# Latent attention: one two-bank score tile, one maximum and one exponential a token tile, and the gates multiplied straight from PSUM

## The chip, the cores and the metric

The kernel runs on one core of a Trainium2 chip. The metric is the device time of one execution in microseconds (us), and lower is better. Three runs of the kernel before gave 3876.71, 3877.76 and 3880.07 us; their median is 3877.76 us.

## The reference, cut to what matters

The whole program is two blocks of two layers each. The first block has a long convolution layer and a grouped attention layer, each followed by an expert layer. The second block has a layer that joins a recurrent unit with a latent attention, and then a state-space layer. The change concerns the latent attention of the second block alone:

```
def _mla_attention(q_nope, q_rope, k_nope, k_rope, v):
    for blk in range(seqlen // Q_BLOCK):              # 8 blocks of 128 tokens
        q0, kend = blk * Q_BLOCK, blk * Q_BLOCK + Q_BLOCK
        s = (einsum('bqhd,bkhd->bhqk', q_nope[:, q0:kend], k_nope[:, :kend])
             + einsum('bqhr,bkr->bhqk', q_rope[:, q0:kend], k_rope[:, :kend])) * scale
        s = where(causal mask, s, -inf)
        p = softmax(s, axis=-1)
        outs.append(einsum('bhqk,bkhd->bqhd', p, v[:, :kend]))
    ...
    y = concatenate([y_rnn, y_mla], axis=-1) * silu(gate)
```

There are 1024 tokens, 8 heads, 64 + 32 columns of query and key a head, and 64 of value. The attention is causal: the tokens of tile t, 128 of them, see (t + 1) x 128 keys.

## The kernel before, in words

Matrices are kept in fp32 and multiplied in three passes: each operand is split into a high part (rounded) and a low part (what is left), and high x high, high x low and low x high are summed. K.split (lines 127 to 134) writes the high part on ScalarE and the low part on VectorE, or on GpSimd where that is asked for.

`mla_attend` (line 1709) runs over 8 heads. For each head it splits the 96-row query and key (line 1722; GpSimd makes the low parts for every head but the first), and then goes over the token tiles in the order 4, 5, 6, 7, 0, 1, 2, 3. Tiles 4 to 7 are the second group of 512 tokens, tiles 0 to 3 the first.

For one tile, `mla_tile` (line 1737) works in parts of 512 keys: one part for tiles 0 to 3, two for tiles 4 to 7. Each part has a PSUM tile of one bank (512 fp32 a partition), from a pool of four (`s=(1, 4)`, line 2260). Three matmuls a part give the scores, and one more with a bf16 mask adds the causal mask on the diagonal block (line 1750). VectorE takes the maximum of each part (line 1755) and, for two parts, the maximum of the two columns, negated (line 1758). ScalarE takes the exponential of each part with that maximum as bias, and writes the part's sum to a column of `sm` (line 1761). `sm` has two rows a tile, one for each part; the second row of tiles 0 to 3 is set to zero (line 1727).

`mla_pT` (line 1764) transposes the tile's probabilities on TensorE, four blocks to a PSUM bank of the pool `tp` (three banks), and splits them into a high part (ScalarE) and a low part (VectorE).

After the last tile of a group, `mla_out` (line 1776) loads the gates of this head and group into the one buffer `ag` (line 1781, on the queue of SP, where the load has to wait until the buffer's last reader is done). It adds the two rows of sums (line 1783), takes reciprocals (line 1784), and turns these columns into rows by four transposes into a `tp` bank (line 1786). ScalarE copies them out of PSUM (line 1788) and GpSimd multiplies them with the gates (line 1789). TensorE multiplies probabilities and values into the one bank of `ov`, ScalarE copies the upper half out (line 1797), VectorE adds the lower (line 1798), GpSimd multiplies with the gated reciprocals (line 1799), and the result is stored over the gates in DRAM (line 1800).

Each engine runs its instructions in one fixed order. The order is not the program's: a planner simulates the engines when the program is built (line 2346, `schedule_with_timeline_sim=True`) and puts each engine's instructions into the order in which they become ready there, earlier program lines first; `K.first(20)` (line 1757) moves an instruction ahead. A buffer taken again waits for all users of the tile that held it (`reuse_waits="tile"`). Heads therefore overlap, and the loads and splits of the next stage's weights (`ProjNorm.weights`, line 1822, tiles `raw`, `pwh`, `pwl`) are placed among the last heads.

Of the kernel before, what the change touches and what calls it, by code (L numbers as in the profile page):

```python
# [10 lines left out]
F32 = mybir.dt.float32  # L11
# [4 lines left out]
OP = mybir.AluOpType  # L16
# [1497 lines left out]
class Ab:  # L1514
# [194 lines left out]
    def mla_attend(self, cp, wk, yT):  # L1709
        K, nc = self.K, self.K.nc  # L1710
        V, G = nc.vector, nc.gpsimd
        idb = cp.tile([P, P], BF16, name="idb")
        V.tensor_copy(out=idb, in_=K.ident)
        z = cp.tile([P, P], BF16, name="zb")
        G.memset(z, 0.0)
        msk = cp.tile([P, P], BF16, name="mskb")
        G.affine_select(out=msk, in_=z, pattern=[[-1, P]], compare_op=OP.is_ge, fill=-1e30, base=0, channel_multiplier=1)
        for h in range(8):
            qk = [wk.tile([96, T], F32R, name=n, tag=n) for n in ("aqh", "aql", "akh", "akl")]
            for s in (slice(0, T),) if h else (slice(0, 512), slice(512, T)):  # L1720
                for i, x in ((2, self.kT), (0, self.qT)):
                    K.split(qk[i][:, s], qk[i + 1][:, s], x[h // 4][0:96, h % 4, s], lo_eng="pool" if h else "dve")
            pp = []
            for tg in range(2):
                pp.append([cp.tile([P, 4 + 4 * tg, 512], F32R, name=f"ap{x}{tg}") for x in "hl"])
            sm = K.small.tile([P, 2, NT], F32, name="asm", tag="asm", bufs=2)
            G.memset(sm[:, 1, 0:4], 0.0)
            todo = [4, 4]
            for t in (4, 5, 6, 7, 0, 1, 2, 3):
                p = self.mla_tile(wk, qk, t, idb, msk, sm)  # L1730
                q = t // 4
                self.mla_pT(p, pp[q], t)
                todo[q] -= 1
                if not todo[q]:
                    self.mla_out(wk, yT, h, q, *pp[q], sm[:, :, 4 * q:4 * q + 4])

    def mla_tile(self, wk, qk, t, idb, msk, sm):

        K, nc = self.K, self.K.nc
        qh, ql, kh, kl = qk  # L1740
        n = (t + 1) * P
        ts = slice(t * P, n)
        parts = []
        for o in range(0, n, 512):
            e = max(o + 256, min(n, o + 512))
            ps = K.psum("as", "s")
            for q, (x, y) in enumerate(((qh, kh), (qh, kl), (ql, kh))):
                K.mm(ps[:, 0:e - o], x[:, ts], y[:, o:e], q == 0, q == 2 and e < n)
            if n <= o + 512:
                K.mm(ps[:, t * P - o:n - o], idb, msk, False, True)  # L1750
            parts.append((o, min(512, n - o), ps))
        m = len(parts)
        mx = K.small.tile([P, 3], F32, name="amx", tag="amx")
        for j, (o, w, ps) in enumerate(parts):
            nc.vector.tensor_reduce(out=mx[:, j:j + 1], in_=ps[:, 0:w], axis=AX.X, op=OP.max, negate=m == 1)
        if m == 2:
            with K.first(20):
                nc.vector.tensor_reduce(out=mx[:, 2:3], in_=mx[:, 0:2], axis=AX.X, op=OP.max, negate=True)
        p = wk.tile([P, 512 * m], F32, name="aprob", tag=f"aprob{m}", bufs=2)
        for j, (o, w, ps) in enumerate(parts):  # L1760
            nc.scalar.activation(out=p[:, o:o + w], in_=ps[:, 0:w], func=AF.Exp, bias=mx[:, 2 * m - 2:2 * m - 1], accum_out=sm[:, j, t:t + 1])
        return p

    def mla_pT(self, p, pp, t):
# [11 lines left out]
    def mla_out(self, wk, yT, h, tg, ph, pl, sm):  # L1776

        K, nc = self.K, self.K.nc
        gt = wk.tile([64, 512], F32, name="ag", tag="ag", bufs=1)
        dst = yT.piece(512 + h * 64, 512 + h * 64 + 64, tg * 512, (tg + 1) * 512)  # L1780
        nc.sync.dma_start(out=gt, in_=dst)
        rs = K.small.tile([P, 4], F32, name="ars", tag="ars", bufs=2)
        nc.vector.tensor_tensor(out=rs, in0=sm[:, 0], in1=sm[:, 1], op=OP.add)
        nc.vector.reciprocal(out=rs, in_=rs)
        rp = K.psum("rT", "tp")
        columns_to_rows(K, rp, rs)
        r = wk.tile([64, 512], F32, name="arb", tag="arb", bufs=1)
        nc.scalar.activation(out=r, in_=rp[0:64, 0:512], func=AF.Copy)
        nc.gpsimd.tensor_tensor(out=gt, in0=r, in1=gt, op=OP.mult)
        po = K.psum("ao", "ov")  # L1790
        nk = tg * 4 + 4
        for k in range(nk):
            c0 = max(0, k - tg * 4) * P
            K.mm(po[:, c0:512], self.v[:, k, h], ph[:, k, c0:512], k == 0, False)
            K.mm(po[:, c0:512], self.v[:, k, h], pl[:, k, c0:512], False, k == nk - 1)
        o = wk.tile([64, 512], F32, name="aoh", tag="aoh", bufs=1)
        nc.scalar.activation(out=o, in_=po[64:128, 0:512], func=AF.Copy)
        nc.vector.tensor_tensor(out=o, in0=po[0:64, 0:512], in1=o, op=OP.add)
        nc.gpsimd.tensor_tensor(out=o, in0=o, in1=gt, op=OP.mult)
        nc.sync.dma_start(out=dst, in_=o)  # L1800
# [439 lines left out]
def recurrent_mla(K, hD, x2D, yT, x0):  # L2240
    ab = Ab(K)
    a = K.a
    with ExitStack() as st:
        with K.staged("right", n=1024, bufs=3), K.pool("mlc", 1, side="right") as lp:
            with K.banks(mm=(2, 2), rg=(2, 1), tp=(1, 2)):
                with K.pool("rnw", 1) as wp, K.pool("u2", 1) as up, K.pool("abv", 1) as vp:
                    uh = up.tile([P, KT, T], F32R, name="uh")
                    ul = up.tile([P, KT, T], F32R, name="ul")
                    with K.pool("mlw", 1, side="right") as lw, K.pool("mp1", 1, side="right") as rp, K.pool("mp2", 2) as wk, K.pool("fn", 1) as fn:
                        w = load_w(K, lw, a["ab_w_in_2"][0], 1536, 416, KT, "m")  # L2250
                        ab.mla_tables(lp, rp)
                        first_norm(K, fn, hD, a["final_norm_g"], uh, ul, x2D, lambda t: t % 2 and ab.mla_latent(w, wk, uh, ul, t - 1), bufs=3, gp=lw, x0=x0)
                    ab.vectors(vp)
                    ab.gate_weights(vp)
                    with K.pool("rnk", 2) as wk:
                        ab.rnn(wk, wp, yT, uh, ul)
            ap = [st.enter_context(K.pool(f"mla{i}", 1)) for i in range(3)]
            with K.banks(mm=(2, 2), tp=(1, 4)), K.pool("mp3", 1) as rp, K.pool("mp4", 2) as wk:
                ab.mla_heads(ap, rp, wk)
        with K.banks(s=(1, 4), tp=(1, 3), ov=(1, 1)), K.pool("mac", 1, side="right") as cp, K.pool("mat", 2, side="right") as wk:  # L2260
            ab.mla_attend(cp, wk, yT)


# [86 lines left out]
```

## Time and profile before

| what | value |
|---|---|
| median of three runs | 3877.76 us |
| the profiled execution | 3875.91 us, span 3874.2 us |
| TensorE busy | 3539.8 us (91%) |
| VectorE busy | 2812.6 us (73%) |
| ScalarE busy | 2082.9 us (54%) |
| GpSimd busy | 1057.2 us (27%) |
| mean granted TensorE clock | 0.959 of full speed |

The profile is one execution, taken by the hardware profiler. Times in it are counted from the first instruction. PE is TensorE's matmuls, PEld its weight loads, DVE is VectorE, ACT is ScalarE, POOL is GpSimd, and SP is the engine whose queue issues the loads and stores. An instruction is named by its line, its operation and "out<-in" with the program's tile names: `as` are scores, `amx` maxima, `aprob` exponentials, `apT`, `aph` and `apl` the transposed probabilities and their parts, `asm` and `ars` the sums and their reciprocals, `rT` and `arb` the reciprocals as rows, `ag` the gates, `ao` and `aoh` the output. In brackets stands how long the engine was idle before an instruction, and what ended it; of several waits the profile names the one that it takes for the last.

### The profile page before, as it was taken

To read this page: it belongs to the slowest core of one execution; us is meant where nothing else is said; L and a number is where in the kernel's file an instruction comes from. 1 tells how busy PE (TensorE), PEld (TensorE's weight loads), DVE (VectorE), ACT (ScalarE), POOL (GpSimd) and SP (SyncE) were. 2 spreads that over 40 slices of the span, in tenths; PEclk is the share of its full clock that TensorE was granted. 3 is DMA by queue.
4 is the path that set the end of the run, shared out by engine and by line. 5 is a ranking of instruction groups with operands and counts; after the bars stand their busy time and mean duration, and the time that the engine had idled before them with its cause. 6 is when DMAs were issued, how large, how long until landed. Compare 5 with 4: busy or idle time off the path is not lost.

```text
span 3874.2 us, 52781 instructions
## 1 busy us (share of the span) xinstructions
PE 3539.8 (91%) x19679; PEld 3004.9 (78%) x19679; DVE 2812.6 (73%) x4848; ACT 2082.9 (54%) x3228; POOL 1057.2 (27%) x939
## 2 busy tenths in 40 slices
PE   7997999985999989899895999979998999999998
PEld 6885878764988979777785988878876877778777
DVE  6547878857988779777777988866476856665565
ACT  4334532222776763689824776754486138665520
POOL 2004755400353321244401453322353000000010
PEclk9998999987999999999997999989999999999999
DMA  4223233454999961000265999951113313232431
GB/s 155 95 83 109 112 132 121 132 200 166 356 361 353 357 221 41 16 12 12 65 225 211 371 354 356 361 177 44 48 34 102 118 41 97 85 95 66 146 139 63
DMA packets 221321, 603.64 MB, mean 156 GB/s; under 512 B 23350, under 2 KB 129704, under 8 KB 195465
## 3 DMA queue, kind: packets, MB, share of 16 engines
q1 hardware_dynamic: 209369, 558.59, 40.0%
q0 software_dynamic: 11696, 41.69, 4.1%
q8 instruction: 155, 2.54, 0.3%
q14 instruction: 101, 0.83, 0.1%
HBM read 503.60 MB, written 96.60 MB: 155 GB/s over the span
## 4 chain that ended last, share of the span: by engine, by line
PE 59%; DVE 11%; ACT 5%; DMA 4%; issue 3%; POOL 1%; SPq 0%; ACTq 0%; DVEq 0%; POOLq 0%
PE out L176 12%; PE gate L176 8%; PE xbc L176 7%; PE up L176 5%; DVE mwl L134 4%; PE down L176 4%; PE z L176 3%; PE ov L176 2%; PE pT L125 2%; PE gs L176 2%; PE as L176 1%; PE yd L176 1%; PE qk L176 1%; PE xr L176 1%; POOL mwl L134 1%
## 5 line engine op out<-in xcount | busy, mean ns | idle before, releaser
L134 DVE TENSOR_TENSOR mwl<-mwr,mwh 128x1024 fp32r<-128x1024 f32 x486 | 644.4, 1377 | 54.5 <-ACT mwh L130 53.6
L130 ACT ACTIVATE mwh<-mwr 128x1024 fp32r<-128x1024 f32 x576 | 562.9, 1050 | 52.6 <-PE up L176 28.8
L134 POOL TENSOR_TENSOR mwl<-mwr,mwh 128x1024 fp32r<-128x1024 f32 x90 | 257.5, 2887 | 271.1 <-ACT mwh L130 252.7
L1857 POOL DMA_DIRECT2D pyr<-y3T_d x31 | 23.5, 758 | 725.2 <-PE z L176 592.2
L1226 POOL DMA_INDIRECT xg<-xn_d,idx x32 | 58.9, 1839 | 466.9 <-DVE gsc L1224 466.3
L915 POOL TENSOR_TENSOR oh<-oh,oh 64x256 f32<-64x256 f32 (+1 forms) x56 | 55.0, 983 | 396.8 <-ACT oh L914 382.4
L134 DVE TENSOR_TENSOR gpl<-pT,gph 128x512 fp32r<-128x512 f32 x168 | 110.7, 685 | 40.6 <-ACT gph L130 26.7
L125 PE MATMUL pT<-ident,prob 128*128 128x128 f32 x896 | 126.7, 276 | 13.9 <-DVE gpl L134 8.6
L873 DVE TENSOR_REDUCE mx<-gs 128x1 f32<-128x1024 f32 x96 | 117.0, 1218 | 30.4 <-PE gs L176 30.0
L176 PE MATMUL gate<-mwh,xgl 128*128 128x384 f32 x512 | 137.2, 349 | 0.6 <-DVE xgl L134 0.4
L125 PEld LDWEIGHTS pT<-ident,prob 128*128 128x128 f32 x896 | 105.2, 141 | 39.9 <-ACT prob L875 6.6
L176 PE MATMUL gate<-mwl,xgh 128*128 128x384 f32 x512 | 134.7, 343 | 0.9 <-DVE mwl L134 0.8
L176 PE MATMUL out<-pwh,pyl 128*128 128x512 f32 x384 | 121.8, 398 | 13.6 <-DVE pyl L134 13.6
L176 PE MATMUL gate<-mwh,xgh 128*128 128x384 f32 x512 | 134.0, 341 | 0.0
L176 PE MATMUL up<-mwl,xgh 128*128 128x384 f32 x512 | 132.0, 337 | 1.9 <-DVE mwl L134 1.9
L176 PE MATMUL up<-mwh,xgh 128*128 128x384 f32 x512 | 132.2, 338 | 0.0
L176 PE MATMUL up<-mwh,xgl 128*128 128x384 f32 x512 | 131.6, 337 | 0.0
L130 ACT ACTIVATE xgh<-xgT 128x512 fp32r<-128x512 f32 (+1 forms) x68 | 38.1, 566 | 173.5 <-PE xgT L125 172.9
L176 PE MATMUL down<-mwl,hh 128*128 128x512 f32 x384 | 122.6, 401 | 6.1 <-POOL mwl L134 6.0
L176 PE MATMUL down<-mwh,hl 128*128 128x512 f32 x384 | 122.9, 400 | 0.0
L176 PE MATMUL out<-pwh,pyh 128*128 128x512 f32 x384 | 121.8, 398 | 0.0
L176 PE MATMUL out<-pwl,pyh 128*128 128x512 f32 x384 | 121.6, 398 | 0.0
(743 smaller groups left out, 11366.0 us busy)
## 6 DMA issues: line engine op xcount, KB each, us to landing
mwr<-in_exp_w_gate_dram SPq DMA_DIRECT2D x64, 1536.0 KB
mwr<-in_exp_w_up_dram SPq DMA_DIRECT2D x64, 1536.0 KB
mwr<-in_exp_w_down_dram SPq DMA_DIRECT2D x64, 1536.0 KB
raw<-in_ssd_w_in_dram SPq DMA_DIRECT2D x40, 512.0 KB
csr<-cs_d SPq DMA_DIRECT2D x32, 512.0 KB
k_d<-kev SPq DMA_DIRECT2D x54, 256.0 KB
kt<-k_d SPq DMA_DIRECT2D x54, 256.0 KB
raw<-in_hy_w_in_dram SPq DMA_DIRECT2D x10, 1024.0 KB
```

What stands on the lines that cost most here:

```text
L125: self.nc.tensor.transpose(out, in_, self.ident[:n, :n])
L130: nc.scalar.activation(out=hi, in_=src, func=AF.Copy)
L134: e.tensor_tensor(out=lo, in0=src, in1=hi.bitcast(F32), op=OP.subtract)
L176: self.nc.tensor.matmul(out=out, lhsT=lhsT, rhs=rhs, start=start, stop=stop)
L873: nc.vector.tensor_reduce(out=mx, in_=ps, axis=AX.X, op=OP.max, negate=True)
L915: nc.gpsimd.tensor_tensor(out=o2, in0=o2, in1=o, op=OP.add)
L1226: nc.gpsimd.indirect_dma_start(out=xg, out_offset=None, in_=self.xnD, in_offset=bass.IndirectOffsetOnAxis(ap=idx[:, 0:1], axis=0))
L1857: K.nc.gpsimd.dma_start(out=raw, in_=yT[q].rearrange("(p k) t -> p k t", k=self.kt)[:, :, t * P:(t + 1) * P])
```

## The change

Tiles 4 to 7 get one PSUM tile of two banks each, from a pool of two (`s=(2, 2)`); tiles 0 and 1 share one such tile, a bank each, and so do tiles 2 and 3. The matmuls are the same and write the same number of columns. One maximum and one exponential then go over the whole width of a tile, up to 1024 columns in two banks. The sums need one row, so the memset and the addition go. VectorE multiplies the transposed reciprocals with the gates straight out of PSUM, in place of ScalarE's copy and GpSimd's multiply.

```diff
-            sm = K.small.tile([P, 2, NT], F32, name="asm", tag="asm", bufs=2)
-            G.memset(sm[:, 1, 0:4], 0.0)
-            todo = [4, 4]
+            sm = K.small.tile([P, NT], F32, name="asm", tag="asm", bufs=2)
             for t in (4, 5, 6, 7, 0, 1, 2, 3):
-                p = self.mla_tile(wk, qk, t, idb, msk, sm)
+                if t > 3 or t % 2 == 0:
+                    ps = K.psum("as", "s")
+                p = self.mla_tile(wk, qk, t, idb, msk, sm, ps if t > 3 else ps[:, t % 2 * 512:t % 2 * 512 + 512])
                 q = t // 4
                 self.mla_pT(p, pp[q], t)
-                todo[q] -= 1
-                if not todo[q]:
-                    self.mla_out(wk, yT, h, q, *pp[q], sm[:, :, 4 * q:4 * q + 4])
+                if t % 4 == 3:
+                    self.mla_out(wk, yT, h, q, *pp[q], sm[:, 4 * q:4 * q + 4])
...
         for o in range(0, n, 512):
             e = max(o + 256, min(n, o + 512))
-            ps = K.psum("as", "s")
             for q, (x, y) in enumerate(((qh, kh), (qh, kl), (ql, kh))):
-                K.mm(ps[:, 0:e - o], x[:, ts], y[:, o:e], q == 0, q == 2 and e < n)
+                K.mm(ps[:, o:e], x[:, ts], y[:, o:e], q == 0, q == 2 and e < n)
             if n <= o + 512:
-                K.mm(ps[:, t * P - o:n - o], idb, msk, False, True)
-            parts.append((o, min(512, n - o), ps))
...
-        for j, (o, w, ps) in enumerate(parts):
-            nc.vector.tensor_reduce(out=mx[:, j:j + 1], in_=ps[:, 0:w], axis=AX.X, op=OP.max, negate=m == 1)
-        if m == 2:
-            with K.first(20):
-                nc.vector.tensor_reduce(out=mx[:, 2:3], in_=mx[:, 0:2], axis=AX.X, op=OP.max, negate=True)
-        p = wk.tile([P, 512 * m], F32, name="aprob", tag=f"aprob{m}", bufs=2)
-        for j, (o, w, ps) in enumerate(parts):
-            nc.scalar.activation(out=p[:, o:o + w], in_=ps[:, 0:w], func=AF.Exp, bias=mx[:, 2 * m - 2:2 * m - 1], accum_out=sm[:, j, t:t + 1])
+                K.mm(ps[:, t * P:n], idb, msk, False, True)
+        mx = K.small.tile([P, 1], F32, name="amx", tag="amx")
+        nc.vector.tensor_reduce(out=mx, in_=ps[:, 0:n], axis=AX.X, op=OP.max, negate=True)
+        p = wk.tile([P, 1024 if t > 3 else 512], F32, name="aprob", tag=f"aprob{t // 4}", bufs=2)
+        nc.scalar.activation(out=p[:, 0:n], in_=ps[:, 0:n], func=AF.Exp, bias=mx, accum_out=sm[:, t:t + 1])
...
-        nc.vector.tensor_tensor(out=rs, in0=sm[:, 0], in1=sm[:, 1], op=OP.add)
-        nc.vector.reciprocal(out=rs, in_=rs)
+        nc.vector.reciprocal(out=rs, in_=sm)
         rp = K.psum("rT", "tp")
         columns_to_rows(K, rp, rs)
-        r = wk.tile([64, 512], F32, name="arb", tag="arb", bufs=1)
-        nc.scalar.activation(out=r, in_=rp[0:64, 0:512], func=AF.Copy)
-        nc.gpsimd.tensor_tensor(out=gt, in0=r, in1=gt, op=OP.mult)
+        nc.vector.tensor_tensor(out=gt, in0=rp[0:64, 0:512], in1=gt, op=OP.mult)
...
-        with K.banks(s=(1, 4), tp=(1, 3), ov=(1, 1)), K.pool("mac", 1, side="right") as cp, K.pool("mat", 2, side="right") as wk:
+        with K.banks(s=(2, 2), tp=(1, 3), ov=(1, 1)), K.pool("mac", 1, side="right") as cp, K.pool("mat", 2, side="right") as wk:
```

## Rows read from the trace of the kernel before

**Rows 1.** The page: its first line.

```profile
span 3874.2 us, 52781 instructions
```

**Rows 2.** Busy time by head period: stretch, us, then PE, PEld, DVE, ACT, POOL; clock; DMA.

```profile
2833.28:2851.98 18.70, 18.36 (x119) 14.96 (x117) 14.39 (x36) 16.37 (x43) 10.11 (x8) 1.00 0.20 57
...
2869.71:2887.34 17.63, 16.85 (x114) 14.22 (x113) 14.16 (x35) 15.69 (x43) 9.94 (x8) 1.00 0.13 32
...
2922.60:2949.72 27.12, 20.21 (x112) 15.98 (x111) 19.49 (x40) 19.30 (x46) 15.15 (x8) 0.87 0.32 98
```

**Rows 3.** Waits of TensorE in the stage: us in total, times, longest.

```profile
PE as L176 <- ACT aprob L1761: 10.5, 7, 6.2
```

**Rows 4.** TensorE in time, steady head: start, us, instruction [idle before].

```profile
2879.14 0.23 PE L176 MATMUL as<-mskb,idb 128*128 128x128 bf16 x1
...
2883.26 0.44 PE L176 MATMUL as<-akh,aqh 96*128 96x384 f32 x1 [0.78 <-ACT aprob L1761]
```

**Rows 5.** ScalarE in time, steady head.

```profile
2877.81 0.59 ACT L1788 ACTIVATE arb<-rT 64x512 f32<-64x512 f32 x1
...
2878.28 0.59 ACT L130 ACTIVATE aph<-apT 128x512 fp32r<-128x512 f32 x1
...
2882.43 0.69 ACT L1761 ACTIVATE aprob<-as,amx 128x512 f32<-128x512 f32 x1
...
2883.09 0.70 ACT L1761 ACTIVATE aprob<-as,amx 128x512 f32<-128x512 f32 x1
...
2883.75 0.38 ACT L1761 ACTIVATE aprob<-as,amx 128x128 f32<-128x128 f32 x1
```

**Rows 6.** VectorE in time, steady head.

```profile
2879.86 0.68 DVE L1755 TENSOR_REDUCE amx<-as 128x1 f32<-128x512 f32 x1
...
2880.66 0.14 DVE L1758 TENSOR_REDUCE amx<-amx 128x1 f32<-128x2 f32 x1
```

**Rows 7.** ScalarE, TensorE and GpSimd in time, the period from 2922.60.

```profile
2939.66 1.06 ACT L130 ACTIVATE pwh<-raw 128x1024 fp32r<-128x1024 f32 x1 [4.37 <-DMA raw<-in_ab_w_out_dram]
...
2943.30 0.69 PE L176 MATMUL as<-akh,aqh 96*128 96x384 f32 x1 [6.18 <-ACT aprob L1761]
...
2929.41 4.46 POOL L1799 TENSOR_TENSOR aoh<-aoh,ag 64x512 f32<-64x512 f32 x1 [0.90 <-POOL asm L1727]
```

**Rows 8.** ScalarE in time, the other attention of the kernel.

```profile
1703.74 1.10 ACT L875 ACTIVATE prob<-gs,mx 128x1024 f32<-128x1024 f32 x1
...
1704.83 0.58 ACT L130 ACTIVATE gph<-pT 128x512 fp32r<-128x512 f32 x1
```

**Rows 9.** Groups by form, 2815 to 2978: busy us, mean ns; idle before.

```profile
L1755 DVE TENSOR_REDUCE amx<-as 128x1 f32<-128x512 f32 x48 | 32.5, 681 | 6.7 <-PE as L176 6.7
...
L1798 DVE TENSOR_TENSOR aoh<-ao,aoh 64x512 f32<-64x512 f32 x15 | 10.1, 675 | 2.5 <-ACT aoh L1797 2.4
...
L1783 DVE TENSOR_TENSOR ars<-asm 128x4 f32<-128x4 f32 x16 | 5.7, 359 | 1.6 <-ACT aprob L1761 1.1
...
L1758 DVE TENSOR_REDUCE amx<-amx 128x1 f32<-128x2 f32 x32 | 4.5, 140 | 0.3
```

**Rows 10.** The page's group of 1024-wide maxima, the other attention.

```profile
L873 DVE TENSOR_REDUCE mx<-gs 128x1 f32<-128x1024 f32 x96 | 117.0, 1218 | 30.4 <-PE gs L176 30.0
```

**Rows 11.** GpSimd, then the DMA queue, in time, steady head.

```profile
2876.51 1.26 POOL L1799 TENSOR_TENSOR aoh<-aoh,ag 64x512 f32<-64x512 f32 x1 [0.90 <-POOL asm L1727]
...
2881.15 1.28 POOL L1789 TENSOR_TENSOR ag<-arb,ag 64x512 f32<-64x512 f32 x1 [3.37 <-ACT aprob L1761]
...
2878.30 0.60 SPq L1781 DMA_DIRECT2D ag<-yT  x1
...
2884.47 0.60 SPq L1781 DMA_DIRECT2D ag<-yT  x1
```

**Rows 12.** VectorE in time, the stage's tail.

```profile
2973.54 1.02 DVE L1783 TENSOR_TENSOR ars<-asm 128x4 f32<-128x4 f32 x1
...
2978.55 0.68 DVE L1798 TENSOR_TENSOR aoh<-ao,aoh 64x512 f32<-64x512 f32 x1 [2.74 <-ACT aoh L1797]
```

More of the change, by code (lines that the diff above doesn't have):

```diff
@@ L1725, in mla_attend, with mla_tile @@
                 pp.append([cp.tile([P, 4 + 4 * tg, 512], F32R, name=f"ap{x}{tg}") for x in "hl"])
-            sm = K.small.tile([P, 2, NT], F32, name="asm", tag="asm", bufs=2)
-            G.memset(sm[:, 1, 0:4], 0.0)
-            todo = [4, 4]
+            sm = K.small.tile([P, NT], F32, name="asm", tag="asm", bufs=2)
             for t in (4, 5, 6, 7, 0, 1, 2, 3):
-                p = self.mla_tile(wk, qk, t, idb, msk, sm)
+                if t > 3 or t % 2 == 0:
+                    ps = K.psum("as", "s")
+                p = self.mla_tile(wk, qk, t, idb, msk, sm, ps if t > 3 else ps[:, t % 2 * 512:t % 2 * 512 + 512])
                 q = t // 4
                 self.mla_pT(p, pp[q], t)
-                todo[q] -= 1
-                if not todo[q]:
-                    self.mla_out(wk, yT, h, q, *pp[q], sm[:, :, 4 * q:4 * q + 4])
-    def mla_tile(self, wk, qk, t, idb, msk, sm):
+                if t % 4 == 3:
+                    self.mla_out(wk, yT, h, q, *pp[q], sm[:, 4 * q:4 * q + 4])
+    def mla_tile(self, wk, qk, t, idb, msk, sm, ps):
         K, nc = self.K, self.K.nc
@@ L1742, in mla_tile @@
         ts = slice(t * P, n)
-        parts = []
         for o in range(0, n, 512):
             e = max(o + 256, min(n, o + 512))
-            ps = K.psum("as", "s")
             for q, (x, y) in enumerate(((qh, kh), (qh, kl), (ql, kh))):
-                K.mm(ps[:, 0:e - o], x[:, ts], y[:, o:e], q == 0, q == 2 and e < n)
+                K.mm(ps[:, o:e], x[:, ts], y[:, o:e], q == 0, q == 2 and e < n)
             if n <= o + 512:
-                K.mm(ps[:, t * P - o:n - o], idb, msk, False, True)
-            parts.append((o, min(512, n - o), ps))
-        m = len(parts)
-        mx = K.small.tile([P, 3], F32, name="amx", tag="amx")
-        for j, (o, w, ps) in enumerate(parts):
-            nc.vector.tensor_reduce(out=mx[:, j:j + 1], in_=ps[:, 0:w], axis=AX.X, op=OP.max, negate=m == 1)
-        if m == 2:
-            with K.first(20):
-                nc.vector.tensor_reduce(out=mx[:, 2:3], in_=mx[:, 0:2], axis=AX.X, op=OP.max, negate=True)
-        p = wk.tile([P, 512 * m], F32, name="aprob", tag=f"aprob{m}", bufs=2)
-        for j, (o, w, ps) in enumerate(parts):
-            nc.scalar.activation(out=p[:, o:o + w], in_=ps[:, 0:w], func=AF.Exp, bias=mx[:, 2 * m - 2:2 * m - 1], accum_out=sm[:, j, t:t + 1])
+                K.mm(ps[:, t * P:n], idb, msk, False, True)
[3 more added lines that the diff above has]
+        nc.scalar.activation(out=p[:, 0:n], in_=ps[:, 0:n], func=AF.Exp, bias=mx, accum_out=sm[:, t:t + 1])
         return p
```

## The prediction, made before the result was known

> **What bounds the kernel now.** I read the head of the page first, then the attention stage by head, then the waits of TensorE there, then each engine's instructions in order of time through one steady head. The span is 3874.2 us [rows 1]; the profiled execution took 3875.91 us, so 1.71 us lie around the span, and it stands 1.85 us under the median of the runs shown (3877.76). The change touches one stage, the latent attention, from 2815 to 2978 us, some 160 us or 4% of the span. Whatever the change does, it can only give back what TensorE loses there.
>
> Cut at the four transposes of each head's first reciprocals, the stage falls into head periods [rows 2]. Three periods in a row are 17.63 us (one of them is shown) with TensorE busy 16.85, ScalarE 15.69, VectorE 14.16, GpSimd 9.94. TensorE is the pace, idle 0.78 us a head, and ScalarE is close behind. Two periods are odd: the first takes 18.70, and the one from 2922.60 takes 27.12, 9.49 over a steady one. Over the stage TensorE waits 10.5 us for an exponential before a score matmul, 7 times [rows 3], its longest wait by far.
>
> In a steady head that wait has one place [rows 4]: the scores of tile 2 (96x384) stand 0.78 us for a bank that tile 7 still holds. The bank comes free with the exponential of tile 7's first half, started 2882.43, its second half at 2883.09 [rows 5]. That exponential was not waiting for its maximum, ready at 2880.80 [rows 6]; ScalarE did a copy of an output half and two splits of transposes first.
>
> The 27.12 us period has another cause: ScalarE stands 4.37 us for the next stage's raw weights, with exponentials queued behind it, and TensorE stands 6.18 us for one of these [rows 7]. The weights' DMA was late because the output multiply on GpSimd took 4.46 us there [rows 7] instead of 1.26 [rows 11].
>
> **The change, part by part.** TensorE keeps every matmul and transpose, so its 16.85 us a head are untouched.
>
> *ScalarE.* Four tiles a head (4 to 7) lose one of two exponentials, one accumulator read with it. For tile 7 the two halves take 2 x 0.66 = 1.32 us from start to start [rows 5]; one 1024-wide exponential with its read takes 1.09 in the other attention of this kernel (1703.74 to 1704.83) [rows 8]. That saves 0.23; the same fixed part goes from tiles 4 to 6, so 4 x 0.23 = 0.92 a head. The two copies of the reciprocals out of PSUM go: 0.47 from start to start [rows 5], so 0.94. Together 1.86 us of ScalarE's 15.69 a head.
>
> *VectorE.* A 512-wide maximum costs 681 ns, the two-column one 140 [rows 9], a 1024-wide one 1218 [rows 10]. Tile 7: 681 + 681 + 140 - 1218 = 284 saved; what goes in tiles 4 to 6 is the same, one instruction's fixed part and the two-column one. Four tiles: 1.14 us. The two additions of partial sums go, 2 x 0.359 = 0.72. The gate multiply comes, twice; its nearest row is the 64x512 addition of the output halves, which also has one operand in PSUM, 675 ns [rows 9], so 1.35. Net 0.5 us a head less.
>
> *GpSimd.* Two multiplies of 1.28 us go, 2.56 a head [rows 11], and a memset. It is at 9.94 of 17.63, so this by itself is worth nothing; the output multiply that follows waits for VectorE's sum of the output halves.
>
> What of this is on the path? Only what moves TensorE's 0.78 us. Two things pull on it. The maximum of tile 7 is now one instruction that starts when both halves are scored: TensorE's last matmul of them starts 2879.14 and takes 0.23 [rows 4], so 2879.37 plus 1.22 gives 2880.6, no later than the 2880.80 of before [rows 6]. But the bank now comes free only after the whole exponential, 1.09 instead of 0.66 us after its start, 0.43 later. Against that ScalarE has 0.23 less in tile 6's exponential just ahead, and, being free sooner, may take tile 7 before the two splits. If it does, the exponential runs from about 2881.1 to 2882.2 and TensorE, free at 2882.48, doesn't wait: the stall goes, -0.78. If it keeps the order, the stall grows by 0.43 - 0.23 = 0.20. I take a little past the middle, -0.3 a head, for the eight heads less the two odd ones: -1.8 us, with ends -4.7 and +1.2.
>
> The coarser release of the score buffers elsewhere (two tiles of two banks in place of four of one) I cost at nothing: the widest tile holds its buffer for six score matmuls, each under 0.5 us [rows 4], a maximum of 1.22 [rows 10] and an exponential of 1.09 [rows 8], 5.3 us at most; three tiles share a buffer in a head, two of them narrower, and these fit into 17.63. What covers it is the transposes and output matmuls between. If that cover fails once a head, it costs one exponential's half, 0.43 x 8 = 3.4.
>
> *The new wait.* The gate load is issued after the output multiply of the group before has read the one gate buffer. In the steady head that multiply starts 2876.51, the load is issued 2878.30, and its landing starts the old gate multiply at 2881.15 [rows 11] (the row names an exponential, but ScalarE's copy, the multiply's other input, had ended at 2878.40 [rows 5], so it was the load). Before, ScalarE copied the transposed reciprocals of the group of tiles 0 to 3 out at 2877.81 [rows 5] and GpSimd, with nothing urgent behind, stood for the load. Now VectorE stands for it, with every maximum and low-part subtraction behind, and the transposes keep one of three transpose banks 3.3 us longer. The load for tiles 4 to 7 is on time: issued at 2884.47 [rows 11], by the same 2.85 us it lands at 2887.32, when that group's transposes are just starting (2887.34, the end of the steady period [rows 2]). Bounds a head: nothing, if the multiply is queued beside the sum of the output halves, which comes later anyway; 2881.15 + 0.6 - 2879.86 = 1.9 us, if it is queued ahead of tile 7's maximum [rows 6]. A planner that counts the load's time would put it late, so I am near the lower end: +0.2 a head, +1.6 over eight.
>
> Here a rule of the Trainium skill speaks against the change. The trace has an in-order engine held by a load: ScalarE's 4.37 us stand with ready work behind it [rows 7]. The page "TensorE: Matmul & The Clock Gate", section "Architectural detail: the array is 16× 32×32, not 1× 128×128", calls ScalarE and VectorE strict first-in-first-out queues; by that rule alone no later maximum may pass the multiply, which is the slower rival below, while the row only says what such a hold costs once it has happened.
>
> *The 27.12 us period* I leave as it is, cost 0: neither the weights' loads and splits nor the output multiply that is slow there is edited. Ends: -9.5 if it vanishes, +5 if the late load and the gate wait add up.
>
> *The tail.* After the last exponential the addition of partial sums takes 1.02 us [rows 12] (contention; the mean is 0.359), and the last subtractions that TensorE needs stand behind it on the same engine. It goes: -1.0. The new multiply there falls into VectorE's 2.74 us of idle before 2978.55 [rows 12], cost 0; without that cover 0.7.
>
> Sum: -1.8 + 1.6 - 1.0 = -1.2, and the first period's surplus of 1.07 [rows 2], half of it from exponentials, gives another -0.5: -1.7 us. 3875.91 - 1.7 = 3874.2 profiled, 3876.0 as a median.
>
> **The rivals.**
> A (forecast, 0.51): TensorE keeps the pace, gain and gate wait nearly cancel: 3876, its own range 3870 to 3883.
> B, faster (0.25): the per-head stall goes whole and the lighter ScalarE and GpSimd let the weights through earlier in the odd period. 6 x 0.78 + 1.0 + half of 9.5 = 10.4: 3867; all of it, 15: 3863. For: ScalarE at 89% loses 12% of its work. Against: the exponential of tile 7 waited on order, not on a full engine, and the weights' load depends on GpSimd's collision.
> C, slower (0.18): the gate load takes the place of the exponential as what ends TensorE's wait. VectorE stands at the multiply for tiles 0 to 3 of each head from about 2879.4 until the load lands; tile 7's maximum comes up to 1.9 us later, its exponential about 1.5 past the old start. 1.5 x 8 - 1.5 of gains = +10.5: 3888. It decides from the point where the multiply is queued before a maximum whose scores are ready earlier than the landing. For: the landing is 3.34 us behind the start of the copy that it replaces. Against: VectorE idles 3.47 us a head and may absorb it.
> D, the change doesn't do what it says (0.06): the two small tiles that share one buffer are tracked as one, so the second tile's scores wait for the first's exponential: a narrow exponential of 0.38 [rows 5], a maximum of less and the handovers, some 1.0 us, x 2 pairs x 8 = 16: 3894. Nothing in the trace of before speaks on it: its score buffers had one tile each.
>
> **How the numbers follow.** About 0.2%, 7.8 us, is what a measurement of this kernel can tell from no change: 3870.0 to 3885.5. B is faster (0.25), A is same (0.51), C and D are slower (0.24). The range, 3866 to 3889, leaves out the far part of B and most of D. The likeliest case's own range stands with A.
>
> **What would show it.** Right: steady periods of 17.2 to 17.8 us with the same 16.85 of TensorE; 64 exponentials in place of 96; ScalarE near 13.8 a head; the multiply near 0.67 us. Step on tile 7 wrong: no wait of TensorE for an exponential, or one above 1 us. Gate step wrong: VectorE shown waiting for the gate's DMA over 0.5 us a head. The odd period: its length against 27.12. I am wrong altogether if the steady period leaves 16.8 to 18.2, or if time outside 2815 to 2990 us changes.

## The result, and the profile after

The changed kernel takes 3907.88 us (median of 6 runs, 3905.73 to 3919.48) against 3878.91 for the kernel before (median of 6): ratio 1.008, 95% interval 1.007 to 1.009. It is slower by about 29 us, outside the predicted range. The profiled execution took 3905.77 us.

The page's first line [rows 1]:

```profile
span 3904.1 us, 52641 instructions
```

Nearly the whole loss lies in the attention stage: what lies ahead of it takes as long as before, what lies behind it 1.9 us more. Next, busy time by stretch in each kernel, from the first score matmul to the first product of the stage behind, and what follows. Columns as in [rows 2]; first the kernel before, then the changed one.

```profile
2815.50:2982.40 166.90, 145.08 (x897) 118.61 (x897) 127.13 (x284) 135.70 (x347) 83.03 (x54) 0.94 0.19 53
...
2982.37:3874.20 891.83, 864.83 (x4533) 687.52 (x4533) 563.25 (x823) 409.21 (x598) 24.07 (x34) 0.98 0.30 97
```

```profile
2815.30:3010.40 195.10, 156.96 (x896) 129.08 (x896) 128.73 (x220) 124.58 (x267) 58.24 (x32) 0.89 0.16 46
...
3010.40:3904.10 893.70, 866.47 (x4533) 687.05 (x4533) 563.00 (x823) 409.39 (x598) 24.06 (x34) 0.99 0.30 97
```

The stage is 28.2 us longer. ScalarE, VectorE and GpSimd didn't become the bound: ScalarE is 11.1 us lighter, GpSimd 24.8. TensorE has the same matmuls (896 records for 897) and two losses: it is idle 38.1 us instead of 21.8 (+16.3), and busy 156.96 instead of 145.08 (+11.9), at a granted clock of 0.89 instead of 0.94. So one part is waiting and the other is the same work at a lower clock.

Four head periods of the changed kernel, cut as in [rows 2] at the reciprocals of tiles 4 to 7; the first, third and fourth answer to the three rows there.

```profile
2833.03:2854.45 21.42, 18.09 (x120) 14.97 (x119) 15.07 (x28) 14.25 (x33) 7.24 (x4) 1.00 0.11 26
2854.45:2875.55 21.10, 17.27 (x114) 14.42 (x112) 14.36 (x27) 14.57 (x33) 7.21 (x4) 1.00 0.25 76
...
2898.00:2922.00 24.00, 20.09 (x114) 16.79 (x113) 14.68 (x27) 14.50 (x33) 7.18 (x4) 0.86 0.09 23
2945.71:2970.95 25.24, 20.78 (x113) 16.94 (x111) 17.95 (x30) 17.93 (x36) 7.17 (x4) 0.86 0.27 82
```

A period from the middle of the stage is 24.00 us instead of 17.63, far past the 18.2 from which the prediction calls itself wrong altogether: 3.13 us more idle (3.91 for 0.78) and 3.24 more busy. (No period is as steady as before: the seven take 21.10 to 25.24 us. The second idles 3.83 us, nearly as long as the one shown, but at a clock of 1.00. The steady head of the changed kernel, below, is the one from 2898.00.) The odd period of 27.12 is 25.24, hardly longer than its neighbours. What TensorE waits for (waits of the stage; answers to [rows 3]), and the one wait of VectorE that the gate step spoke of:

```profile
PE apT L125 <- ACT aprob L1751: 23.5, 11, 2.9
PE apT L125 <- DVE apl L134: 6.7, 8, 1.1
...
PE as L176 <- ACT aprob L1751: 0.3, 1, 0.3
...
DVE ag L1776 <- DMA ag<-yT: 1.1, 2, 0.7
```

The wait of score matmuls for a free bank, 10.5 us before, is gone (0.3). In its place the transposes of probabilities wait for their exponential, 23.5 us (2.6 before). TensorE in order of time through the longest of these in the steady head (answers to [rows 4]):

```profile
2900.42 0.40 PE L176 MATMUL as<-akh,aqh 96*128 96x512 f32 x1
...
2902.78 0.52 PE L125 MATMUL apT<-ident,aprob 128*128 128x128 f32 x3
2903.05 0.47 PE L176 MATMUL as<-akh,aqh 96*128 96x512 f32 x1
...
2903.82 0.23 PE L176 MATMUL as<-mskb,idb 128*128 128x128 bf16 x1
2906.74 1.11 PE L125 MATMUL apT<-ident,aprob 128*128 128x128 f32 x4 [2.69 <-ACT aprob L1751]
2907.51 0.77 PE L176 MATMUL as<-akh,aqh 96*128 96x512 f32 x1
2908.08 0.63 PE L176 MATMUL as<-akl,aqh 96*128 96x512 f32 x1
```

The matmuls from 2903.05 on are tile 3's scores, right behind the transposes of tile 2; TensorE ends them at 2904.05, and next in its order are the transposes of this same tile. The next head's first scores, at 2900.42, were put ahead of them. In the kernel before it was the other way round; these are the first score matmuls there of tile 3 and of the next head:

```profile
2884.65 0.48 PE L176 MATMUL as<-akh,aqh 96*128 96x512 f32 x1
...
2885.46 0.48 PE L176 MATMUL as<-akh,aqh 96*128 96x512 f32 x1
```

There tile 3's scores began 1.39 us after tile 2's [rows 4], and TensorE had the next head's to do while VectorE and ScalarE dealt with tile 3. ScalarE over the same time (answers to [rows 5]), with the wide exponential of tile 7 at the end:

```profile
2900.54 0.57 ACT L1751 ACTIVATE aprob<-as,amx 128x384 f32<-128x384 f32 x1
2901.00 0.20 ACT L1751 ACTIVATION_READ_ACCUMULATOR aprob<-as,amx 128x1 f32 x1
...
2904.03 1.04 ACT L130 ACTIVATE aqh<-mqT 96x1024 fp32r<-96x1024 f32 x1
2904.98 1.04 ACT L130 ACTIVATE akh<-mkT 96x1024 fp32r<-96x1024 f32 x1
2905.92 0.67 ACT L1751 ACTIVATE aprob<-as,amx 128x512 f32<-128x512 f32 x1
...
2918.49 1.11 ACT L1751 ACTIVATE aprob<-as,amx 128x1024 f32<-128x1024 f32 x1 [0.28 <-DVE amx L1749]
...
2919.60 0.36 ACT L1751 ACTIVATE aprob<-as,amx 128x128 f32<-128x128 f32 x1
```

Tile 3's scores come after tile 2's exponential (2900.54 to 2901.20), though they lie in another bank. Then two splits of query and key, 1.89 us from start to start, go ahead of tile 3's exponential. And busy time of two stretches right around the stall shows the clock:

```profile
2898.00:2903.80 5.80, 5.80 (x36) 4.88 (x34) 2.71 (x7) 3.00 (x9) 0.00 (x0) 1.00 0.00 1
2906.74:2912.60 5.86, 5.86 (x22) 5.17 (x23) 2.59 (x5) 2.79 (x6) 3.63 (x2) 0.50 0.18 45
```

Ahead of the stall TensorE runs at 1.00, its level of 2.4 GHz; behind 2.69 us of standing still it gets 0.50, the level of 1.2 GHz, for the next 5.86 us, and a 96x512 score matmul takes 0.63 to 0.77 instead of 0.39 to 0.47.

Why the second tile of a pair waits stands in the order of TensorE's instructions in the program as built (line, instruction, and in brackets the semaphore that it waits for: PE_49 is TensorE's own, Activation_49 ScalarE's; a tile of the program has a number). Here for the pair 0 and 1, both in the tile as_27191:

```
L176 MATMUL as_27191<-akh_27050,aqh_27048 128x256
...
L176 MATMUL as_27217<-akh_27050,aqh_27048 128x384 [waits PE_49]
...
L176 MATMUL as_27191<-akh_27050,aqh_27048 128x256 [waits Activation_49]
```

The first line is tile 0, the last tile 1: it waits for a semaphore of ScalarE, the signal that the exponential of tile 0 is done, and tile 2's scores (as_27217) are put ahead of it. For the pair 2 and 3 no wait is written at tile 3's scores: they stand right behind the transposes of tile 2, which already wait for tile 2's exponential. The two tiles of a pair write different banks and no value passes between them; the wait goes by the shared tile. The Trainium skill ("Perfetto Trace Analysis", section "Matmuls") advises to rotate independent matmul groups through PSUM banks, so that the evacuation of one overlaps the next group. This trace shows that another bank alone does not give that overlap: the second tile has one, and its scores still come after the first's exponential.

### The profile page after: what moved, and what is told of

It reads as the page before. It is cut to its first block, busy times and chain, and to the rows that moved or that the text cites. A ratio compares the mean times of both kernels' runs of the same rounds, so it can differ in the third digit from the quotient of the medians.

```text
span 3904.1 us, 52641 instructions
## 1 busy us (share of the span) xinstructions
PE 3558.5 (91%) x19679; PEld 3022.2 (77%) x19679; DVE 2813.2 (72%) x4784; ACT 2070.9 (53%) x3148; POOL 1034.7 (27%) x915
## 5 line engine op out<-in xcount | busy, mean ns | idle before, releaser
L1844 POOL DMA_DIRECT2D pyr<-y3T_d x31 | 23.5, 758 | 726.5 <-PE z L176 595.2
L873 DVE TENSOR_REDUCE mx<-gs 128x1 f32<-128x1024 f32 x96 | 116.9, 1218 | 30.0 <-PE gs L176 29.6
```

Source lines behind the costliest of these rows:

```text
L873: nc.vector.tensor_reduce(out=mx, in_=ps, axis=AX.X, op=OP.max, negate=True)
L1844: K.nc.gpsimd.dma_start(out=raw, in_=yT[q].rearrange("(p k) t -> p k t", k=self.kt)[:, :, t * P:(t + 1) * P])
```

## The experiments

Each was timed beside the kernel before. Theory 1 is the false wait (rival D of the prediction), rival 2 the coarse buffers and the merge, rival 3 the gate multiply on VectorE.

**1. Both tiles' scores first.**

```diff
                     ps = K.psum("as", "s")
+                    for u in ((t,) if t > 3 else (t, t + 1)):
+                        self.mla_scores(qk, u, idb, msk, ps if t > 3 else ps[:, u % 2 * 512:u % 2 * 512 + 512])
```
(`mla_scores` is the matmul part of `mla_tile`, which then only takes the maximum and the exponential.)

> The changed kernel with one difference: the scores of both tiles of a sharing pair (0 and 1, 2 and 3) are issued before the first maximum of the pair is taken. Theory 1, false wait (two small tiles in one buffer are tracked as one, so the second tile's score matmuls wait for the first one's exponential; that, and the order and the lower clock that follow from it, are the 29 us): most of it comes back, 3877 to 3887 us, and steady head periods fall from 21 to 25 us to about 18. Price paid for the cure: the buffer is full earlier and freed as late as now, 0 to 3 us. Rival 2, coarse buffers (two releases a head and tile in place of four are too few, whoever shares them, and the one maximum over both halves starts too late): 3900 to 3908. Rival 3, the gate multiply on VectorE: 3900 to 3908, since it is kept.

Measured: 3881.59 us, ratio to the kernel before 1.0011 (1.0002 to 1.0019). About 26 of the 29 us are back with nothing changed but the order of issue. A steady head period of it, and TensorE's first score matmul of tiles 0, 1, 2 and 3 there:

```profile
2897.51:2915.70 18.19, 17.34 (x114) 14.25 (x114) 14.17 (x27) 14.35 (x34) 7.29 (x4) 1.00 0.12 30
```

```profile
2903.51 0.39 PE L176 MATMUL as<-akh,aqh 96*128 96x256 f32 x1
2904.01 0.36 PE L176 MATMUL as<-akh,aqh 96*128 96x256 f32 x1
...
2906.87 0.42 PE L176 MATMUL as<-akh,aqh 96*128 96x384 f32 x1
2907.53 0.47 PE L176 MATMUL as<-akh,aqh 96*128 96x512 f32 x1
```

Partners now stand side by side, TensorE idles 0.85 us a head, and the clock is 1.00. Theory 1 is borne out; rivals 2 and 3 as the main cause fall.

**2. The merge undone.** Two maxima and two exponentials for tiles 4 to 7 in the two-bank tile:

```diff
...
-        nc.vector.tensor_reduce(out=mx, in_=ps[:, 0:n], axis=AX.X, op=OP.max, negate=True)
...
+        for j, (o, w) in enumerate(parts):
+            nc.vector.tensor_reduce(out=mx[:, j:j + 1], in_=ps[:, o:o + w], axis=AX.X, op=OP.max, negate=m == 1)
...
+        for j, (o, w) in enumerate(parts):
+            nc.scalar.activation(out=p[:, o:o + w], in_=ps[:, o:o + w], func=AF.Exp, bias=mx[:, 2 * m - 2:2 * m - 1], accum_out=sm[:, j, t:t + 1])
...
```

The maximum of the two columns, the second row of sums with its memset, and the addition of the rows come back too.

> The changed kernel with the merge alone undone: tiles 4 to 7 keep their two-bank buffer, but take two maxima, a maximum of the two columns, and two exponentials, and the sums their second row and the addition, as before. Pairs still share a buffer, the gates are still multiplied from PSUM. Theory 1, false wait: it stays slow, 3900 to 3912 us (ScalarE has some 0.9 us a head more again). The part of rival 2 that blames the one wide maximum and exponential: 3877 to 3885. The part of rival 2 that blames the coarse release: stays at 3900 to 3912, as under theory 1. Rival 3, the gate multiply: stays slow as well.

Measured: 3939.29 us, ratio 1.015 (1.0134 to 1.0166). Slow as theory 1 says, but some 27 us slower than the changed kernel (1.015 against 1.008), which nothing had foretold: in this layout undoing the merge costs that much. One likely reason stands in VectorE's order in the program as built: of a tile's two maxima only the first waits for TensorE and the second follows it at once, where before each half's maximum had a wait of its own, for its own bank. So no half starts early any more, and the two maxima, the small one and two exponentials all come after the last score. A second stands in the trace: the addition of the sums, 0.17 us in the median, takes 3.4 to 3.5 us in five heads. It ends each time as GpSimd's splits of the next query and key end (here 2926.60 to 2931.33), and TensorE waits 7.8 us in five waits for the reciprocals behind it. How much each of the two costs was not tried apart. One head period, and its slow addition:

```profile
2904.18:2931.62 27.44, 21.46 (x113) 17.61 (x113) 18.83 (x37) 15.35 (x40) 7.34 (x5) 0.81 0.08 20
```

```profile
2927.89 3.46 DVE L1781 TENSOR_TENSOR ars<-asm 128x4 f32<-128x4 f32 x1 [0.28 <-ACT aprob L1759]
```

**3. The old gate path in the changed kernel.**

```diff
-        nc.vector.tensor_tensor(out=gt, in0=rp[0:64, 0:512], in1=gt, op=OP.mult)
+        r = wk.tile([64, 512], F32, name="arb", tag="arb", bufs=1)
+        nc.scalar.activation(out=r, in_=rp[0:64, 0:512], func=AF.Copy)
+        nc.gpsimd.tensor_tensor(out=gt, in0=r, in1=gt, op=OP.mult)
```

> The changed kernel with the old path of the gates: ScalarE copies the reciprocals out of PSUM, GpSimd multiplies. Theory 1, false wait: stays slow, 3903 to 3913 us, since the scores are untouched and ScalarE gets its 0.94 us a head back. Rival 2: the same. Rival 3, the gate multiply on VectorE holds the maxima behind it: 3875 to 3885.

Measured: 3915.77 us, ratio 1.0099 (1.0084 to 1.0114). Rival 3 falls: without its multiply the kernel is no faster. It is 2.8 us above theory 1's range, and 7 to 8 us slower than the changed kernel (by the ratios and by the medians).

**4. The new gates alone**, the same three lines the other way round in the kernel before.

> The kernel before with one difference: VectorE multiplies the reciprocals in PSUM with the gates, in place of ScalarE's copy and GpSimd's multiply. Theory 1 and rival 2: the gates are no part of the loss, 3873 to 3881 us (ScalarE has 0.94 us a head less, VectorE 1.35 more, and a wait for the gates' load of some 0.1 us a head as in the changed kernel). Rival 3: most of the loss is here, 3895 to 3908.

Measured: 3876.81 us, ratio 0.9997 (0.9987 to 1.0006). No change that can be told.

**5. A buffer for every tile.**

```diff
-                if t > 3 or t % 2 == 0:
-                    ps = K.psum("as", "s")
-                p = self.mla_tile(wk, qk, t, idb, msk, sm, ps if t > 3 else ps[:, t % 2 * 512:t % 2 * 512 + 512])
+                ps = K.psum("as", "s")
+                p = self.mla_tile(wk, qk, t, idb, msk, sm, ps)
```

> The changed kernel, but every tile takes a two-bank buffer of its own, the narrow ones too: nobody shares, and the two buffers are taken 8 times a head in place of 6. A tile now waits for the exponential of the tile two before it, where the second of a sharing pair waited for that of the tile just before it. Theory 1 (the wait on the tile just before is what costs): most of the 29 us comes back, 3877 to 3890 us. Rival 2 (two coarse buffers are too few): as slow as the changed kernel or slower, 3905 to 3925, since the buffers are held by more tiles.

Measured: 3881.83 us, ratio 1.0006 (0.9996 to 1.0016). The buffers are as coarse as in the changed kernel and taken more often, and the loss is gone: coarse release is not the cause.

**6. Other partners**, 0 with 2 and 1 with 3:

```diff
-                if t > 3 or t % 2 == 0:
+                if t > 3 or t < 2:
                     ps = K.psum("as", "s")
+                    if t < 2:
+                        two = [ps] if t == 0 else two + [ps]
-                p = self.mla_tile(wk, qk, t, idb, msk, sm, ps if t > 3 else ps[:, t % 2 * 512:t % 2 * 512 + 512])
+                p = self.mla_tile(wk, qk, t, idb, msk, sm, ps if t > 3 else two[t % 2][:, t // 2 * 512:t // 2 * 512 + 512])
```

> The changed kernel with the partners of the sharing changed: tiles 0 and 2 share one buffer, 1 and 3 the other. The number of takes (6 a head) and of sharing pairs is that of the changed kernel; only the tile that a second partner waits for is now two before it, as in the run with buffers of their own. Theory 1: 3877 to 3890 us, within some 5 us of that run. Rival 2: 3900 to 3912, as the changed kernel.

Measured: 3882.66 us, ratio 1.0009 (1.0000 to 1.0018). Sharing as such is harmless too, as long as the partner is two tiles back.

**7. One shared bank in the kernel before.** Tiles 0 and 1 in columns 0 to 255 and 256 to 511:

```diff
+                one = K.psum("as", "s") if t == 0 else one if t == 1 else None
...
-            ps = K.psum("as", "s")
+            ps = one if t < 2 else K.psum("as", "s")
+            ps = ps[:, 256:512] if t == 1 else ps
```

> The kernel before, four one-bank buffers, two maxima and two exponentials, old gates, with one difference: tiles 0 and 1 share one bank, columns 0 to 255 and 256 to 511. It adds one false wait a head and takes nothing else away; it even takes one buffer a head less. Theory 1: slower by one wait a head, at least the 1.0 us of a maximum, an exponential and the handovers x 8 = 8 us, at most half of the 29 of the changed kernel with its two pairs: 3886 to 3893 us. Rival 2 (coarse buffers): no change, 3874 to 3882 us.

Measured: 3884.31 us, ratio 1.0015 (1.0006 to 1.0025), 5.8 us with an interval of 2.3 to 9.7. The direction is theory 1's, the size a little under what I had as its least: TensorE has tile 2's scores to put into the wait. Here the two tiles share a bank as well as a tile, so this run prices the wait but doesn't tell the tile from the bank; the changed kernel, where partners lie in different banks, does.

**8. Both tiles' scores first, old gates.** The edit of the third on top of the first.

> The kernel with the scores of a pair issued together (first experiment), with the old path of the gates (ScalarE's copy, GpSimd's multiply). With the false wait gone it prices the gate path again: theory 1 as it stands gives the gates no part, so within 4 us of the first experiment, 3878 to 3886 us; ScalarE has 0.94 us a head more, 7.5 us in all, which would show in full only if ScalarE set the pace there (3889). Rival 3 (the gate multiply holds VectorE): 5 us or more faster than the first experiment, 3870 to 3877.

Measured: 3891.43 us, ratio 1.0032 (1.0020 to 1.0044). My value missed: with the false wait cured the gate path counts, and the other way than rival 3 had it. The new gates save 8 to 10 us there (by the ratios and by the medians). The stage's row for ScalarE's copies and the wait that grew:

```profile
L1784 ACT ACTIVATE arb<-rT 64x512 f32<-64x512 f32 x16 | 9.3, 584 | 3.4 <-PE rT L125 3.3
```

```profile
PE apT L125 <- ACT aprob L1758: 18.8, 14, 1.7
```

TensorE's wait for exponentials is 18.8 us here and 8.2 in the first experiment; the copies cost ScalarE 9.3. That one comes from the other was not tried apart.

**9 and 10. One pair each.** In the ninth only 0 and 1 share (`if t != 1:` in place of `if t > 3 or t % 2 == 0:`), in the tenth only 2 and 3 (`if t != 3:`).

> The changed kernel, but tiles 2 and 3 take a two-bank buffer each; only tiles 0 and 1 still share one. One false wait a head is left of two, in the layout with two coarse buffers. Theory 1 in its simple form (each false wait has its own price, and they add up): half of the 26 us that the cure of both brought back, so 3891 to 3898 us. Theory 1 in its steeper form (one false wait a head is covered by other ready work, as in the kernel before with one shared bank, where it cost 5.8 us; with two a head the cover runs out and the clock falls too): 3880 to 3889 us. Rival 2: 3903 or more.

> The changed kernel, but tiles 0 and 1 take a two-bank buffer each; only tiles 2 and 3 still share one. The last tile of a head is the one that waits; its exponential releases the transposes for which TensorE was seen to wait longest, 2.69 us in a steady head. Simple form of theory 1: 3891 to 3898 us, like its partner, and the two losses add up to about 26. Steeper form: its own loss and the partner's together stay under 20 us. If the place of the longest wait decides: this run alone keeps most of the loss, 3898 to 3908, and its partner 3880 to 3886.

Measured: 3886.83 us for the pair 0 and 1, ratio 1.0022 (1.0011 to 1.0032), 8.5 us over before; 3918.80 for the pair 2 and 3, ratio 1.0101 (1.0085 to 1.0116), 39 us over. The price is not one per wait: the last tile of a head carries most of it. A head period of the tenth, and the stall in it:

```profile
2899.60:2923.65 24.05, 20.01 (x114) 16.75 (x114) 14.57 (x26) 14.28 (x32) 7.43 (x5) 0.85 0.09 23
```

```profile
2920.69 1.11 PE L125 MATMUL apT<-ident,aprob 128*128 128x128 f32 x4 [2.75 <-ACT aprob L1751]
```

It is the changed kernel's steady head again. That this run is another 8 to 11 us slower than the one with both pairs, and over its expected 3898 to 3908, lies largely ahead of the stage: in the profiled execution its first score matmul starts at 2825.45, 10.1 us later than the changed kernel's, and no edit touches what runs before. Why it starts later was not settled. The stage itself is 3.0 us longer than the changed kernel's (198.1 and 195.1).

**11 and 12. Splits on GpSimd.** From the third head on, the high parts of query and key come from GpSimd; in the changed kernel (11) and in the first experiment's (12).

```diff
...
-                    K.split(qk[i][:, s], qk[i + 1][:, s], x[h // 4][0:96, h % 4, s], lo_eng="pool" if h else "dve")
+                    K.split(qk[i][:, s], qk[i + 1][:, s], x[h // 4][0:96, h % 4, s], hi_eng="pool" if h > 1 else "act", lo_eng="pool" if h else "dve")
```

> The changed kernel, with the false waits left in, but from the third head on GpSimd, not ScalarE, writes the high parts of the query and key (two 96x1024 copies a head). They take a buffer that comes free only with the scores of tile 3 two heads before, so they become ready just when tile 3's late scores do, and in the trace of the changed kernel ScalarE runs both, 1.89 us, ahead of tile 3's exponential, for which TensorE then stands 2.69 us in a steady head. If that knock-on is most of the price of the pair 2 and 3 (theory 1 in its last form): the stall falls to under 1 us, 1.9 us in each of five or six heads and part of the clock's loss come back, 3885 to 3898 us. If the late scores alone are the price: 3903 to 3912, TensorE standing as long for the maximum. If GpSimd's copies make the next head's scores late: above 3912, with waits of TensorE for the query and key.

> The first experiment's kernel (the scores of a pair issued together, so no false wait) with the same move of the high parts of query and key to GpSimd. There ScalarE runs these copies after tile 3's exponential has started, so little hangs on them: 3876 to 3884 us if ScalarE's order costs nothing any more; 3868 to 3875 if ScalarE, 1.89 us lighter a head, was still what its remaining waits for exponentials (8.2 us in 10 waits) come from, and this version would beat both kernels; above 3884 if GpSimd makes the next head's scores late.

Measured: 3902.55 us, ratio 1.0059 (1.0045 to 1.0073), and 3893.88 us, ratio 1.0038 (1.0027 to 1.0050). A head of the eleventh kernel, which answers to the changed kernel's steady head, and its stall:

```profile
2899.76:2920.83 21.07, 17.38 (x113) 14.38 (x112) 14.10 (x27) 12.65 (x31) 9.24 (x6) 1.00 0.11 26
```

```profile
2908.43 0.66 PE L125 MATMUL apT<-ident,aprob 128*128 128x128 f32 x4 [1.91 <-ACT aprob L1753]
```

The splits ahead of the exponential are worth 0.78 of the 2.69 us, not 1.9 as I had it; 1.91 are the late scores, a maximum and the exponential, with nothing for TensorE to do meanwhile. So it ended within 0.5 us of the case "the late scores alone". The row shows one more thing: this head idles 3.69 us, nearly as much as the changed kernel's 3.91, but at a clock of 1.00, and takes 21.07 instead of 24.00. The clock, not the waiting, makes most of that difference, as it does between the changed kernel's own second period and its steady one. Not every head of the eleventh is so short: the clock is 0.86 to 1.00 in them, and the kernel as a whole gains 5 us. The twelfth lost 10 to 12 us to the first: with no false wait to mend, the move only costs. That is the range of the expectation's last case, but the cause named there does not show: TensorE has no wait for a split that GpSimd made. TensorE's wait for exponentials there is 15.2 us (8.2 in the first); what delays them I did not find out.

The medians take in the whole program, and the first score matmul starts anywhere from 2815.3 to 2825.5 us in the profiled executions, one of each kernel. The stage alone, from that matmul to the first product of the next stage, leaves that out. (The kernel before, timed beside each group of experiments, had medians of 3876.59 to 3879.31 us.)

| kernel | median, us | its stage in the profiled execution, us |
|---|---|---|
| before | 3878.91 | 166.9 |
| changed | 3907.88 | 195.1 |
| 1, both tiles' scores first | 3881.59 | 170.4 |
| 2, merge undone | 3939.29 | 225.7 |
| 3, old gates | 3915.77 | 197.5 |
| 4, new gates alone | 3876.81 | 170.0 |
| 5, a buffer for every tile | 3881.83 | 169.0 |
| 6, other partners | 3882.66 | 167.3 |
| 7, one shared bank | 3884.31 | 170.4 |
| 8, scores first, old gates | 3891.43 | 178.9 |
| 9, pair 0 and 1 alone | 3886.83 | 178.2 |
| 10, pair 2 and 3 alone | 3918.80 | 198.1 |
| 11, splits on GpSimd | 3902.55 | 190.5 |
| 12, the same, scores first | 3893.88 | 181.6 |

## Why the prediction was wrong

**The step that failed** is the shared tile: the sum has no term for it, so the step puts its wait at nothing. The prediction saw it only as rival D: "the two small tiles that share one buffer are tracked as one, so the second tile's scores wait for the first's exponential", and gave it a chance of 0.06 and 3894 us. The chance was too small, and the price too low by 14 us. That nothing in the trace of before spoke on it was a reason for an open chance, not for a small one: the description of the planner says that a buffer taken again is waited for by tile, and the edit puts two users into one tile. The price was a sum of equal terms, 1.0 us x 2 pairs x 8 = 16. The term of the pair 0 and 1, 8 us, fits its measured 8.5 (11.3 by the stage; 5.8 in the kernel before). The term of the pair 2 and 3, 8 us as well, measured 39 alone, of which 31 lie in the stage. The two don't add up either: both pairs together cost 28 in the stage, less than the second alone. What I left out of it:
- The place in TensorE's order. Tile 1's late scores leave tile 2's to fill the wait. With tile 3's the next head's scores are the filling; they go ahead while tile 3 waits for tile 2's exponential, and nothing is left behind it but its own transposes. So the latency of its maximum and exponential is bare: 1.91 us even with ScalarE free.
- What slips in. ScalarE's two splits get ahead of the late exponential: 0.78 more.
- The clock. Of the stage's 28.2 us, 16.3 are idle time, by chance the very 16 of rival D; the other 11.9 are the same matmuls at a lower granted clock, 0.50 right behind the stall of the steady head.

**The rest of the sum** did much better, as the runs without the false wait show: 3881.59, 3881.83 and 3882.66 us, each within 0.2% of before, against the forecast's 3876. The cancelling of small gains and small costs was right to that measure; its single terms came out so:
- Coarser release, cost 0: right (fifth and sixth runs).
- Tile 7 and the wider operations: the stall for a free bank went. A 1024-wide maximum took 1222 ns (1218 taken), tile 7's exponential 1.11 us from start to start (1.09 taken). There are 64 exponentials, as predicted, but ScalarE came to 14.50 us a head rather than 13.8. VectorE, taken for 0.5 us lighter a head, was not: 14.68 us in the steady head and 14.17 in the first experiment's, after 14.16. The sum added up durations, but VectorE's instructions overlap in the trace: behind the maximum of 0.68 us at 2879.86 [rows 6] the next one starts at 2880.46.
- The gate wait, +1.6 over the stage: VectorE waited 1.1 us for the gates. Rival C falls. The new multiply, estimated at 675 ns from the addition:

```profile
L1776 DVE TENSOR_TENSOR ag<-rT,ag 64x512 f32<-64x512 f32 x16 | 10.9, 679 | 1.6 <-DMA ag<-yT 1.1
```

- The tail, -1.0: from the start of the last read of an exponential's sum to the first product of the next stage it took 9.07 us before (2973.30 to 2982.37) and 8.12 after (3002.28 to 3010.40), 0.95 less.
- The odd period, cost 0: the output multiply there took 1.26 us in place of 4.46 [rows 7], and the period of 25.24 is 1.24 over a steady one, not 9.49. That would have been rival B's gain, but the runs without the false wait speak against it: in the first experiment this period takes 26.71 us, 8.5 over a steady one, with TensorE waiting 4.7 us for an exponential there, and 22.93 and 21.99 in the fifth and sixth.
- Steady periods without the false wait were 18.19 us (first experiment), not 17.2 to 17.8: the gains of ScalarE did not reach TensorE, whose transposes still wait for exponentials, 8.2 us over that stage.

## What to carry to other kernels

Before two independent users are put into one buffer, ask by what unit the framework tracks it; if by tile, as here, the second user waits for the first one's last reader, though it writes another bank. Either issue all writers before the first reader or share with a partner further back, which cost nothing that could be told here. Price a new wait by its place in the waiting engine's order: the same kind of wait cost 8.5 us (11 in the stage) where other work followed, and 39 (31 in the stage) where only its own consumers did.

## What the runs showed beside this

The length of one stall does not tell what the clock does next. The changed kernel's stall of 2.69 us that ended at 2906.74 was followed by 5.86 us at 0.50. Another of 2.69 us, which ended at 2863.19, was followed by as long a stretch at 1.00:

```profile
2863.19:2869.05 5.86, 5.86 (x40) 5.25 (x41) 3.74 (x6) 3.31 (x7) 3.66 (x2) 1.00 0.71 225
```

In the eleventh kernel the stretch behind the stall of 1.91 us, 2908.43 to 2913.57, ran at 1.00, and the 5.80 us behind one of 1.90 us, from 2951.17 on, at 0.71. What decides it, no run here takes apart. So the price of a wait has a part, the clock, that can't be read from the wait's length alone.

And the two halves of the change lean on each other: the gates from PSUM were worth nothing that could be told in the kernel before, 7 to 8 us in the changed kernel (2.4 in the stage), and 8 to 10 us (8.5 in the stage) where the false wait was gone.
